# Two standing attention lanes with portioned operand loads in a one-core hybrid decoder layer

## The chip, the core and the metric

One core of one Trainium2 chip runs the whole layer in one launch. The metric is the device time of one execution in microseconds; the time before is the median of three executions. The engines are named as the profile names them: PE (TensorE; PEld its weight loads), DVE (VectorE), ACT (ScalarE), POOL (GpSimd), and SP (SyncE), which here only issues DMAs. Each engine works through its own list of instructions in a fixed order and waits where the next one's inputs are not there yet.

## What is computed

One layer on 256 tokens of width 2048. A norm and one wide projection feed two token mixers, whose outputs are gated, projected, merged and projected once more:

```python
h = rmsnorm(x, pre_norm_g[l]); proj = h @ w_in[l]
(a_q, a_k, a_v, a_g, a_lr, b_q, b_k, b_v, b_g, m_a, m_b) = jnp.split(proj, offsets, axis=-1)
o_a = gla_chunked(a_q, a_k, a_v, gk)                 # gated linear attention, 4 heads
y_a = (rmsnorm(o_a) * silu(a_g)) @ w_branch_a[l]
# differential attention, 16 heads, each with two maps of head size 64:
s = einsum('bqhmd,bkhmd->bhmqk', q / 8, k)            # m = 0, 1
p = softmax(where(mask, s, -inf)); w = p[m=0] - lam * p[m=1]; o_b = w @ v
y_b = (rmsnorm(o_b) * (1 - lam_init) * silu(b_g)) @ w_branch_b[l]
merged = sigmoid(m_a) * y_a + sigmoid(m_b) * y_b
x = x + rmsnorm(merged @ w_out[l], post_norm_g[l])
```

## The kernel before

**The stream of weights.** All weights come from DRAM in tiles of 1 MB, called raw, in one written order, `seq`. Each half of a raw tile is split into a rounded part hi (ACT, line 263) and a remainder lo (DVE, line 264), and the products hi*hi, hi*lo and lo*hi are summed on PE (line 451). raw, hi and lo have three buffers each, so a half can be split only when PE has done with the half three places ahead. Before the attention the projections of the first head groups are computed in a long pinned phase, and their queries and keys (heads groups 0 and 1) and the values and gates of all four groups (`gspill`) are spilled to DRAM. After it the order is: the linear mixer's gates, merge gate m01, queries and keys of group 2, m02, group 3, m03, then the branch matrices `y0` and `y1` and the output matrix `o`.

**The attention beside it.** Small work runs as generators in a list `tasks`; `pump(2)`, called after every second half (every tile) of the stream, lets the first two generators take one step each. The last steps of the linear mixer (`gla_scores`, `gla_out`) come first in that list; then come eight `diff_pair` generators, two heads each, group by group. A pair waits until both pairs of the group ahead are done (or until the linear mixer's two outputs are), then loads its operands in one step, waits two steps, and takes five more:

- `scores`: for each of two maps a PSUM bank `bg`; 8 matmuls per head (lines 991, 992) with q2 against kh and kl; DVE adds the causal mask and takes the row maximum (line 996, `prob<-bg`), which empties the bank; ACT takes the exponentials (line 1002);
- `combine` (line 1007 on): DVE forms p0 - lam*p1;
- `turned`: three transposes and a copy; `weighted`: the product with the values, the per-head norm and the gate (lines 1026 to 1039).

Of the two heads of a pair the second is one step behind the first, and the two pairs of a group are one step apart. At the end four transposes (line 1049) turn the result, and `split_out` writes `obh`, `obl` for the matrix `y1`.

**Operands.** q2 holds for map m the rounded queries in one half of the 128 partitions and their remainders in the other half (four DMAs of 64 partitions by `place`); kh and kl hold rounded keys and remainders in both halves (two DMAs each by `twice`). So one matmul of q2 with kh gives two of the four partial products, and one with kl the other two. All of these DMAs, the values (dv) and gates (ub) and the raw tiles go through SP's one queue.

**Buffers.** q2, kh, kl, dv and ub come from a pool of 18 tiles, in which the input x keeps 8 until m03 is done. The tag `bg` has four PSUM banks. A scheduler fixes each engine's order when the program is built.

Of the kernel before, what the change touches and what calls it, by code (L numbers as in the profile page):

```python
# [7 lines left out]
F32R = mybir.dt.float32r  # L8
BF16 = mybir.dt.bfloat16
U8 = mybir.dt.uint8  # L10
AF = mybir.ActivationFunctionType
# [3 lines left out]
P = 128  # L15
# [22 lines left out]
def chunk_plan():  # L38

    plan = [("v0", "two", "w_in", [(6144, RANK), (2048, 2 * VG[0] - RANK)])]  # L40
    at = 2 * VG[0] - RANK
    for g, n in enumerate(VG[2:]):
        plan.append((f"v{g + 2}", "tok", "w_in", [(2048 + at, n)]))
        at += n
    for hf in range(2):
        for name, base in (("k", 1024), ("q", 0)):
            for c in range(4):
                plan.append((f"{name}{hf}{c}", "chan", "w_in", [(base + 512 * hf + P * c, P)]))
    o = 6144 + RANK
    for s in range(2):  # L50
        plan.append((f"set{s}", "set", "w_in", [(o + 10240 + 1024 * s, 1024)]))
    for s in range(2, SETS):
        plan.append((f"set{s}", "set", "w_in", [(o + base + 512 * (s - 2), 512) for base in (4096, 6144)]))
    for g in range(4):
        plan.append((f"ag{g}", "tok", "w_in", [(4096 + 512 * g, 512)]))
        if g + 2 >= SETS:
            plan.append((f"dv{g}", "tok", "w_in", [(o + 4096 + 512 * g, 512)]))
            plan.append((f"bg{g}", "tok", "w_in", [(o + 6144 + 512 * g, 512)]))
# [36 lines left out]
def hybrid_kernel(ctx: ExitStack, tc, xt, xn, preg, postg, w, w2, gkb, glag, lamv, diffg, ident_d, causal_d, lmask_d, out):  # L95
# [36 lines left out]
    def fetch(d, name, make, queue=pool):  # L132
        t = make(list(d.shape), name, d.dtype)
        queue.dma_start(t, d)
        return t
# [5 lines left out]
    def f32(ap):  # L141
        return ap.bitcast(F32)
# [10 lines left out]
    def halves_of(*keys):  # L153
        return [(key, r, h) for key in keys for r in range(len(at[key])) for h in range(2)]

    def heads_order(g):
        values = (f"dv{g}", f"bg{g}") if g + 2 >= SETS else ()
        chans = [] if g in EARLY else [f"{name}{g}{c}" for pair in range(2) for name in ("dq", "dk") for c in (2 * pair, 2 * pair + 1)]
        return halves_of(*values, *chans)

    seq = halves_of("v0", "v2", "v3") + phase_steps()
    seq += halves_of(*(f"ag{g}" for g in range(4)), "m01") + heads_order(0) + heads_order(1) + heads_order(2)
# [493 lines left out]
    gspill = [None] * (2 * SETS)  # L656

    def merge_gate(banks):
        t = u([P, 2, 512], "mgate")
        for b in range(2):  # L660
            act.activation(t[:, b, :], banks[b], AF.Tanh, scale=half_rstd[:, b : b + 1])
        m0.append(spill(t, "mgate"))
# [284 lines left out]
            tasks.append(gla_out(g // 2, gates[g - 1 :]))  # L947


    obh, obl = [], []  # L950

    def place(t, d, m, h):
        sp.dma_start(f32(t[64 * h : 64 * h + 64, m]), d[64 * m : 64 * m + 64])

    def twice(t, d):

        for h in range(2):
            rows = slice(64 * h, 64 * h + 64)
            sp.dma_start(f32(t[rows]), d.rearrange("(m p) i t -> p m i t", m=2))

    def diff_pair(g, pair, values):
        oh, ol = obh[g], obl[g]
        cm = causal.rearrange("p a t -> p (a t)")
        cuts = ((0, P), (P, 3 * P))
        while not {f"pair{g - 1}{p}" if g else f"out{p}" for p in range(2)} <= done:
            yield
        if not values:
            values.extend(fetch(gspill[2 * g + 4 + i], name, u, sp) for i, name in enumerate(("dv", "ub")))
        q2, kh, kl = (u([P, 2, 2, S], name, F32R) for name in ("q2", "kh", "kl"))
        for m in range(2):  # L970
            for h in range(2):
# [5 lines left out]
        vv, uu = values  # L977
        heads_of = [dict(h=2 * pair + i) for i in range(2)]
        og = []

        def scores(w):
            i2 = w["h"] % 2
# [36 lines left out]

        def weighted(w):  # L1020
            h, z, wt = w["h"], w["z"], w["wt"]
            if not og:
                og.append(t2([P, 2, 2, P], "ogb"))
# [17 lines left out]
        one, two = heads_of  # L1041
        for work in (((scores, one),), ((combine, one), (scores, two)), ((turned, one), (combine, two)), ((weighted, one), (turned, two)), ((weighted, two),)):
            for part, w in work:
                part(w)
            yield
        bank = ps("bg")
        for i in range(2):
            for b in range(2):
                pe.transpose(bank[:, P * (2 * i + b) : P * (2 * i + b) + P], og[0][:, i, b, :], ident)
        hi = oh[:, 2 * pair : 2 * pair + 2, :].rearrange("p h t -> p (h t)")  # L1050
        lo = ol[:, 2 * pair : 2 * pair + 2, :].rearrange("p h t -> p (h t)")
        split_out(bank, hi, lo, diffg_s)
        done.add(f"pair{g}{pair}")

    def diff_heads(g):
        values = []
        if g + 2 >= SETS:
            banks = token_major(f"dv{g}", 512, x_ops, 2)
            late_u = u2 if g > 1 else u
            vv = late_u([P, 2, 512], "dv")  # L1060
            for b in range(2):
                act.activation(vv[:, b, :], banks[b], AF.Copy, scale=rstd[:, b : b + 1])
            banks = token_major(f"bg{g}", 512, x_ops, 2)
            uu = late_u([P, 2, 512], "ub")
            for b in range(2):
                gate(banks[b], b, uu[:, b, :])
            values += vv, uu
        make = u2 if g < 2 else u
        obh.append(make([P, 4, S], "obh", F32R))
        obl.append(make([P, 4, S], "obl", F32R))  # L1070
        for pair in range(2):
            for name in () if g in EARLY else ("dq", "dk"):
# [5 lines left out]
            tasks.append(diff_pair(g, pair, values))  # L1078


    def a_ops(kt):
# [8 lines left out]
    for g in range(3):  # L1090
        diff_heads(g)
    merge_gate(token_major("m02", 512, x_ops, 2))
    diff_heads(3)
    merge_gate(token_major("m03", 512, x_ops, 2))
# [180 lines left out]
```

## Time and profile before

| what | value |
|---|---|
| median of three executions | 1111.01 us (1110.8 to 1115.99) |
| the profiled execution itself | 1114.24 us |
| its span, first to last instruction | 1112.5 us |
| mean granted PE clock in it | 0.995 |
| PE busy / DVE / ACT / POOL, share of the span | 99% / 75% / 60% / 11% |
| HBM read / written | 248.40 MB / 25.17 MB |

The profiled execution is one of its own and not one of the three; what lies around its span is 1114.24 - 1112.5 = 1.74 us. A row of a timeline gives start, duration, engine, line, the tile written and read, the count, and in brackets how long the engine had waited and for what. "Busy" counts the time in which an instruction was on the engine; matmuls overlap, so the pace of PE is read from the starts of successive rows.

### The profile page before, as it was taken

Reading aid. Unit: us, or ns where it says so; the run is one execution under the profiler, and the core shown is the slowest. Engines: PE = TensorE matmul, PEld = TensorE weight load, DVE = VectorE, ACT = ScalarE, POOL = GpSimd, SP = SyncE. Lnnn points to the kernel's source line nnn. Section 1 sums busy time; section 2 is a strip of 40 time slices with the busy share of each in tenths; the row PEclk is TensorE's granted clock in tenths of the full one; section 3 lists DMA queues with packets and bytes.
Section 4 is the critical chain, followed back from the end, with each engine's and each line's share of the span. In section 5 each row is a group of like instructions: output and inputs, shape, how many; then the busy total and the mean of one; then the engine's idle time right before and its main releaser. Section 6 shows DMA issues by size and latency. Waiting matters only on the chain.

```text
span 1112.5 us, 15209 instructions
## 1 busy us (share of the span) xinstructions
PE 1098.4 (99%) x5546; PEld 943.9 (85%) x5546; DVE 839.3 (75%) x1176; ACT 666.9 (60%) x975; POOL 120.7 (11%) x185
## 2 busy tenths in 40 slices
PE   9999999999999999999999999999999899999997
PEld 8999888888888888888888888889888788888886
DVE  7797977979979889799898757758675655656463
ACT  7885766666666766667555455747574643444460
POOL 0201111121121210220100001011100010000000
PEclk9999999999999999999999999999999899999999
DMA  9869879699797897984845679869949575556752
GB/s 346 291 227 327 279 267 306 163 302 295 276 304 205 318 252 256 317 243 157 331 158 184 222 244 288 260 214 304 297 171 263 200 282 189 189 189 212 272 196 77
DMA packets 57884, 274.56 MB, mean 247 GB/s; under 512 B 7440, under 2 KB 8976, under 8 KB 38352
## 3 DMA queue, kind: packets, MB, share of 16 engines
q1 hardware_dynamic: 37536, 192.57, 49.7%
q0 software_dynamic: 19264, 79.70, 25.2%
q10 hardware_dynamic: 1008, 1.32, 0.4%
q8 instruction: 43, 0.70, 0.2%
q14 instruction: 33, 0.27, 0.1%
HBM read 248.40 MB, written 25.17 MB: 246 GB/s over the span
## 4 chain that ended last, share of the span: by engine, by line
PE 97%; ACT 1%; DVE 1%; issue 1%; DMA 0%; DVEq 0%; SPq 0%; POOLq 0%; POOL 0%; ACTq 0%
PE mm L451 66%; PE bg L451 19%; PE bg L439 2%; PE mm L424 2%; PE mm L439 2%; PE bg L870 1%; PE bg L424 1%; PE bg L992 1%; PE bg L991 1%; DMA raw<-in_w_dram 0%; PE bg L1016 0%; PE bg L1027 0%; PE bg L1028 0%; PE bg L1026 0%; PE bg L1124 0%
## 5 line engine op out<-in xcount | busy, mean ns | idle before, releaser
L263 ACT ACTIVATE hi<-raw 128x1024 fp32r<-128x1024 f32 (+3 forms) x291 | 299.6, 1032 | 319.9 <-PE mm L451 216.9
L264 DVE TENSOR_TENSOR lo<-raw,hi 128x1024 fp32r<-128x1024 f32 (+3 forms) x291 | 345.3, 1190 | 179.5 <-ACT hi L263 176.5
L451 PE MATMUL mm<-hi,xs 128*128 128x512 f32 (+1 forms) x864 | 217.3, 387 | 0.3 <-ACT hi L263 0.3
L451 PEld LDWEIGHTS mm<-hi,xs 128*128 128x128 f32 x864 | 159.7, 188 | 27.1 <-ACT hi L263 0.7
L451 PE MATMUL bg<-xs,hi 128*128 128x512 f32 x512 | 131.9, 389 | 0.0
L264 DVE TENSOR_TENSOR lo<-a,hi 128x1024 fp32r<-128x1024 f32 x96 | 115.7, 1220 | 8.1 <-ACT hi L263 7.0
L451 PE MATMUL mm<-lo,xs 128*128 128x512 f32 (+1 forms) x432 | 119.1, 384 | 0.1
L263 ACT ACTIVATE hi<-a 128x1024 fp32r<-128x1024 f32 x96 | 101.7, 1060 | 22.8 <-PE mm L451 20.4
L451 PEld LDWEIGHTS bg<-xs,hi 128*128 128x128 f32 x512 | 96.2, 188 | 18.7
L451 PEld LDWEIGHTS mm<-lo,xs 128*128 128x128 f32 x432 | 80.9, 188 | 15.1 <-DVE lo L264 0.4
L451 PEld LDWEIGHTS bg<-xs,lo 128*128 128x128 f32 x512 | 69.8, 190 | 5.0
L451 PE MATMUL bg<-xs,lo 128*128 128x256 f32 x512 | 71.4, 282 | 0.0
L451 PE MATMUL mm<-xs,hi 128*128 128x512 f32 x256 | 66.9, 394 | 0.0
L264 DVE TENSOR_TENSOR lo<-b,hi 128x1024 fp32r<-128x1024 f32 x48 | 57.8, 1221 | 7.4 <-ACT hi L263 6.6
L263 ACT ACTIVATE hi<-b 128x1024 fp32r<-128x1024 f32 x48 | 50.8, 1060 | 15.6 <-PE mm L451 13.8
L451 PE MATMUL mm<-hi,oah 128*128 128x512 f32 x128 | 52.0, 406 | 3.0 <-ACT hi L263 3.0
L451 PEld LDWEIGHTS mm<-xs,hi 128*128 128x128 f32 x256 | 46.2, 189 | 7.8
L451 PE MATMUL mm<-hi,oal 128*128 128x512 f32 x128 | 51.1, 399 | 0.0
L451 PE MATMUL mm<-hi,obh 128*128 128x512 f32 x128 | 50.4, 394 | 0.0
L451 PE MATMUL mm<-hi,obl 128*128 128x512 f32 x128 | 49.9, 390 | 0.0
L1002 ACT ACTIVATE prob<-prob,mx,score_scale 128x128 f32<-128x128 f32 x64 | 34.1, 534 | 15.9 <-DVE mx L997 15.9
L451 PE MATMUL mm<-hi,mh 128*128 128x512 f32 x96 | 37.5, 390 | 0.0
(286 smaller groups left out, 1866.1 us busy)
## 6 DMA issues: line engine op xcount, KB each, us to landing
raw<-in_w_dram SPq DMA_DIRECT2D x128, 1024.0 KB, 5.3
a<-in_w_dram POOLq DMA_DIRECT2D x24, 512.0 KB, 12.7
c<-in_w_dram SPq DMA_DIRECT2D x24, 512.0 KB, 8.7
b<-in_w_dram POOLq DMA_DIRECT2D x24, 512.0 KB, 9.1
raw<-in_w_dram SPq DMA_DIRECT2D x14, 832.0 KB, 7.1
a<-in_w_dram POOLq DMA_DIRECT2D x10, 1024.0 KB, 5.2
b<-in_w_dram POOLq DMA_DIRECT2D x10, 1024.0 KB, 7.8
dh<-dh POOLq DMA_DIRECT2D x16, 256.0 KB, 4.3
```

The source lines that it names most:

```text
L263: act.activation(hi_t[:, a:b], r[:, a:b], AF.Copy)
L264: dve.tensor_tensor(out=lo_t[:, a:b], in0=r[:, a:b], in1=f32(hi_t[:, a:b]), op=ALU.subtract)
L424: i = pe.matmul(out, lhs, rhs, start=first and n == 0, stop=last and n == len(pairs) - 1)
L439: i = pe.matmul(banks[g][b][:, :n], a[part][:, P * b : P * b + P], w[:, n * g : n * g + n], start=first, stop=last)
L451: i = pe.matmul(*args, **kw)
L870: pe.matmul(o, xk[:, P * c : P * c + P], xq.rearrange("p (b c t) -> p b c t", b=2, c=4)[:, :, c, :], start=i == 0, stop=i == 1)
L991: pe.matmul(banks[m][:, lo:up], q2[:, m, i2, t], kh[:, m, i2, :n], start=True, stop=False)
L992: pe.matmul(banks[m][:, lo:up], q2[:, m, i2, t], kl[:, m, i2, :n], start=False, stop=True)
L1002: act.activation(prob[m][:, lo:up], prob[m][:, lo:up], AF.Exp, scale=score_scale[:, b : b + 1], bias=mx[:, i : i + 1], accum_out=z[:, i : ...
```

## The change

The eight pairs become two generators, `diff_lane(0)` and `diff_lane(1)`, one for each pair of every group, which live through all four groups:

- Each lane has one q2, one kh and one kl for good, and clears one half of kl per map once (POOL memset). Into kl only the half that meets the rounded queries is loaded, so the product of remainder with remainder is left out of the scores. A pair has then 4 + 4 + 2 = 10 DMAs of 64 partitions and 128 KB, 1.25 MB; it had 4 of 128 KB and 4 of 256 KB, 1.5 MB.
- After the second head's scores the lane is given the three portions "q", "kh", "kl" of the next group, and `arrive` loads one of them at each of the next steps.
- A lane does not wait for the other lane or for the group to be done. The transposes of a group's result (`turned_out`) run at the start of the next group's first step; the five-step pairs of a lane follow each other directly.
- dv is fetched in that first step and ub in the second, by lane 0. Merge gates m01 to m03 come from another pool, and `obh`, `obl` are made only when they are needed.
- The branches for groups that are computed late, which never applied with `SETS = 6`, are gone. The matrix products and their order in the stream stay as they were.

```diff
+    def diff_lane(pair):
...
+        while not {"scores1", "out0"} <= done:
+            yield
         q2, kh, kl = (u([P, 2, 2, S], name, F32R) for name in ("q2", "kh", "kl"))
         for m in range(2):
-            for h in range(2):
-                place(q2, heads[g, pair, "dq"][h != m], m, h)
-        for t, d in zip((kh, kl), heads[g, pair, "dk"]):
-            twice(t, d)
-        yield
-        yield
+            pool.memset(f32(kl[64 - 64 * m : P - 64 * m, m]), 0.0)
+        missing = []
+        def arrive(g):
+            if not missing or (g, pair, "dk") not in heads:
+                return
+            part = missing.pop(0)
+            for m in range(2):
+                for h in range(2):
+                    if part == "q":
+                        place(q2, heads[g, pair, "dq"][h != m], m, h)
+                    elif part == "kh":
+                        place(kh, heads[g, pair, "dk"][0], m, h)
+                    elif h == m:
+                        place(kl, heads[g, pair, "dk"][1], m, h)
...
+        for g in range(4):
...
+            one, two = (dict(g=g, h=2 * pair + i) for i in range(2))
+            if pair == 0:
+                values[g] = [fetch(gspill[2 * g + 4], "dv", u, sp)]
+            if g:
+                turned_out(g - 1)
+            scores(one)
+            yield
+            if pair == 0:
+                values[g].append(fetch(gspill[2 * g + 5], "ub", u, sp))
+            combine(one)
+            scores(two)
+            yield
+            missing += ("q", "kh", "kl") if g < 3 else ()
+            for work in (((turned, one), (combine, two)), ((weighted, one), (turned, two)), ((weighted, two),)):
+                arrive(g + 1)
+                for part, w in work:
+                    part(w)
+                yield
+        turned_out(3)
+    tasks.extend(diff_lane(pair) for pair in range(2))
```

What the scheduler makes of it shows at three places. (The changed program's lines are numbered 5 lower in the stream's functions, 3 lower where a tile is fetched, and 7 lower in `scores`; numbers behind a name tell tiles apart.)

**SP, the operands of the last group.** Before, in the middle of `y0`, 18 DMAs stand between the raw tiles 7898 and 7943: one of dv, and the 17 shown here, ub and the two pairs' q, kh and kl:

```order
L134 DMA ub_7879<-gr_4702 128x1024
L953 DMA q_752_7881<-dh_6873 64x512
L953 DMA q_752_7881<-dl_6875 64x512 x2
L953 DMA q_752_7881<-dh_6873 64x512
L959 DMA kh_7882<-dh_7062 64x2x512 x2
L959 DMA kl_7883<-dl_7064 64x2x512 x2
L953 DMA q_759_7932<-dh_7227 64x512
L953 DMA q_759_7932<-dl_7229 64x512 x2
L953 DMA q_759_7932<-dh_7227 64x512
L959 DMA kh_7933<-dh_7371 64x2x512 x2
L959 DMA kl_7934<-dl_7373 64x2x512 x2
L226 DMA raw_7943<-in_w_dram 128x2048
```

Now the same group's operands (dv, and the lanes' q, kh and kl) stand around the last tiles of m03 and the first one of `y0`, 7653, a portion of each lane at a time:

```order
L131 DMA dv_7687<-gl_4789 128x1024
L221 DMA raw_7504<-in_w_dram 128x2048
L948 DMA q_488_6140<-dh_6924 64x512
L948 DMA q_488_6140<-dl_6926 64x512 x2
L948 DMA q_488_6140<-dh_6924 64x512
L948 DMA kh_6141<-dh_7105 64x512 x4
L221 DMA raw_7577<-in_w_dram 128x2048
L948 DMA q_497_6206<-dh_7296 64x512
L948 DMA q_497_6206<-dl_7298 64x512 x2
L948 DMA q_497_6206<-dh_7296 64x512
L948 DMA kl_6142<-dl_7107 64x512 x2
L221 DMA raw_7653<-in_w_dram 128x2048
```

The last two portions follow behind 7653. The largest number of operand DMAs between two raw tiles is now 14, at group 2. The last group is through 14 halves (7 tiles) of the stream earlier than before.

**ACT, the last group's exponentials.** Before, in the middle of `y0`, the splits of tile 7943 stood behind seven exponentials of two heads (763 and 764 are the two maps of the one, 771 and 772 of the other):

```order
L1002 ACTIVATE prob_763_7977,z_7980<-prob_763_7977,mx_7979,score_scale 128x128
L1002 ACTIVATE prob_763_7977,z_7980<-prob_763_7977,mx_7979,score_scale 128x256
L1002 ACTIVATE prob_764_7978,z_7980<-prob_764_7978,mx_7979,score_scale 128x128
L1002 ACTIVATE prob_764_7978,z_7980<-prob_764_7978,mx_7979,score_scale 128x256
L1002 ACTIVATE prob_771_8039,z_8042<-prob_771_8039,mx_8041,score_scale 128x128
L1002 ACTIVATE prob_771_8039,z_8042<-prob_771_8039,mx_8041,score_scale 128x256
L1002 ACTIVATE prob_772_8040,z_8042<-prob_772_8040,mx_8041,score_scale 128x128
L263 ACTIVATE hi_7961<-raw_7943 128x1024
L263 ACTIVATE hi_8002<-raw_7943 128x1024
```

Now this group meets the end of m03 and the first tiles of `y0` (7653, 7738). Their splits 7740 and 7756 stand behind the first head's four exponentials, of which two rows are shown, and ahead of the second head's (735):

```order
L995 ACTIVATE prob_723_7699,z_7701<-prob_723_7699,mx_7700,score_scale 128x128
L995 ACTIVATE prob_723_7699,z_7701<-prob_723_7699,mx_7700,score_scale 128x256
L258 ACTIVATE hi_7740<-raw_7653 128x1024
L258 ACTIVATE hi_7756<-raw_7738 128x1024
L656 ACTIVATE mgate_7832<-mm_7502,half_rstd 128x512
L656 ACTIVATE mgate_7832<-mm_7503,half_rstd 128x512
L498 ACTIVATE obh_7694<-bg_7802,diffg_s 128x512
L995 ACTIVATE prob_735_7779,z_7782<-prob_735_7779,mx_7781,score_scale 128x128
```

Between the two heads' exponentials stand two splits, the merge gate and a result's hi part, where before nothing stood.

**PE and DVE, two heads' scores in one step.** Before, at group 2, the scores of two heads followed each other on PE in four banks, 7522, 7523, 7545 and 7546:

```order
L992 MATMUL bg_7522<-kl_7359,q_674_7357 128x256
L991 MATMUL bg_7523<-kh_7358,q_674_7357 128x256
L992 MATMUL bg_7523<-kl_7359,q_674_7357 128x256
L991 MATMUL bg_7545<-kh_7412,q_683_7411 128x128
L992 MATMUL bg_7545<-kl_7413,q_683_7411 128x128
L991 MATMUL bg_7546<-kh_7412,q_683_7411 128x128
L992 MATMUL bg_7546<-kl_7413,q_683_7411 128x128
```

Now, at group 3, a bank of transposes (7802) stands between them, so the step uses five; with four banks the fifth, 7814, is one that 7783 or 7784 has left:

```order
L985 MATMUL bg_7783<-kl_6142,q_488_6140 128x256
L984 MATMUL bg_7784<-kh_6141,q_488_6140 128x256
L985 MATMUL bg_7784<-kl_6142,q_488_6140 128x256
L1039 MATMUL bg_7802<-ident,ogb_7632 128x128 x4
L984 MATMUL bg_7813<-kh_6207,q_497_6206 128x128
L985 MATMUL bg_7813<-kl_6208,q_497_6206 128x128
L984 MATMUL bg_7814<-kh_6207,q_497_6206 128x128
```

At group 1 the order is the same, but the fifth bank (6903) comes behind all four matmuls of the fourth (6902) and four of the stream; at group 2 likewise, with six of the stream:

```order
L1039 MATMUL bg_6891<-ident,ogb_6693 128x128 x4
L984 MATMUL bg_6902<-kh_6207,q_497_6206 128x128
L985 MATMUL bg_6902<-kl_6208,q_497_6206 128x128
L984 MATMUL bg_6902<-kh_6207,q_497_6206 128x256
L985 MATMUL bg_6902<-kl_6208,q_497_6206 128x256
L446 MATMUL mm_6929<-xs_75,hi_6743 128x512 x2
L446 MATMUL mm_6929<-xs_76,hi_6743 128x512 x2
L984 MATMUL bg_6903<-kh_6207,q_497_6206 128x128
```

On DVE at group 3 the reductions that empty banks 7783 and 7784 stand behind two splits of weights:

```order
L259 TENSOR_TENSOR lo_7741<-raw_7653,hi_7740 128x1024
L259 TENSOR_TENSOR lo_7757<-raw_7738,hi_7756 128x1024
L989 ISA prob_735_7779,mx_7781<-bg_7783,causal 128x128
L989 ISA mx_7781 128x1
L989 ISA prob_735_7779,mx_7781<-bg_7783,causal 128x256
```

At groups 1 and 2 one split and one small operation on queries or keys stand there. PE has 3784 rows in both programs, with the same matmuls.

More of the change, by code (lines that the diff above doesn't have):

```diff
@@ L1021, in weighted @@
             h, z, wt = w["h"], w["z"], w["wt"]
-            if not og:
-                og.append(t2([P, 2, 2, P], "ogb"))
+            if h % 2 == 0:
+                og[:] = [t2([P, 2, 2, P], "ogb")]
+            vv, uu = values[w["g"]]
             bank = ps("bg")
@@ L1039, in weighted @@
                 dve.scalar_tensor_tensor(out=og[0][:, h % 2, b, :], in0=bank[:, P * b : P * b + P], scalar=e[:, b : b + 1], in1=uu[:, b, hv], op0=ALU.mult, op1=ALU.mult)
[L1041 to L1044, printed above, removed]
-            yield
[L1046 to L1053, printed above, removed]
-    def diff_heads(g):
[L1056 to L1070, printed above, removed]
+        def turned_out(g):
+            bank = ps("bg")
+            for i in range(2):
+                for b in range(2):
+                    pe.transpose(bank[:, P * (2 * i + b) : P * (2 * i + b) + P], og[0][:, i, b, :], ident)
+            if len(obh) == g:
+                make = u2 if g < 2 else u
+                obh.append(make([P, 4, S], "obh", F32R))
+                obl.append(make([P, 4, S], "obl", F32R))
+            hi = obh[g][:, 2 * pair : 2 * pair + 2, :].rearrange("p h t -> p (h t)")
+            lo = obl[g][:, 2 * pair : 2 * pair + 2, :].rearrange("p h t -> p (h t)")
+            split_out(bank, hi, lo, diffg_s)
@@ new lines, in diff_lane @@
+        for g in range(4):
+            if g == 0:
+                missing += "q", "kh", "kl"
+            late = len(missing)
+            while missing:
+                arrive(g)
+                yield
+            if late:
+                yield
+            while "out1" not in done:
+                yield
[5 more added lines that the diff above has]
+            scores(one)
+            yield
+            if pair == 0:
[8 more added lines that the diff above has]
+                    part(w)
+                yield
@@ L1089, in hybrid_kernel @@
     merge_gate(token_major("m01", 512, x_ops, 2))
-    for g in range(3):
-        diff_heads(g)
+    diff_heads(2)
     merge_gate(token_major("m02", 512, x_ops, 2))
```

27 lines of the change are left out of this document (5 added, 22 removed).

## Prediction, made before the changed kernel ran

> **What bounds the kernel now.** I read the page first: the busy shares, the slices, the chain that ended last.
>
> ```profile
> span 1112.5 us, 15209 instructions
> PE 1098.4 (99%) x5546; PEld 943.9 (85%) x5546; DVE 839.3 (75%) x1176; ACT 666.9 (60%) x975; POOL 120.7 (11%) x185
> PE   9999999999999999999999999999999899999997
> PEclk9999999999999999999999999999999899999999
> PE 97%; ACT 1%; DVE 1%; issue 1%; DMA 0%; DVEq 0%; SPq 0%; POOLq 0%; POOL 0%; ACTq 0%
> ```
>
> PE is busy for 1098.4 of 1112.5 us and holds 97% of the chain; DMA holds none of it. Only one slice of forty before the last, number 32 (about 862 to 890 us), shows PE below nine tenths, and there its clock is lower too. The change keeps every matmul, so whatever it gains must come out of PE's idle time and of that clock. Next come the waits of PE alone (waiting line, releaser: us in total, times, longest), and the stretches around slice 32 (length, then busy time of PE, PEld, DVE, ACT and POOL with counts, PE clock, DMA share, GB/s):
>
> ```profile
> PE mm L451 <- ACT hi L263: 3.4, 2, 3.0
> PE bg L345 <- DVE ones_b L342: 1.6, 1, 1.6
> PE bg L439 <- ACT hi L263: 0.7, 1, 0.7
> ```
>
> ```profile
> 840.00:860.00 20.00, 20.00 (x96) 16.71 (x95) 10.73 (x23) 7.89 (x15) 1.79 (x3) 1.00 1.06 293
> 860.00:880.00 20.00, 16.95 (x76) 14.03 (x75) 14.25 (x47) 11.12 (x25) 0.00 (x0) 0.83 0.69 261
> 880.00:900.00 20.00, 20.00 (x109) 17.15 (x108) 12.20 (x28) 12.54 (x35) 3.53 (x6) 1.00 0.52 182
> ```
>
> Of the long stream one wait is left: 3.05 us for a rounded half, hi. Its neighbours have none. The timeline shows who was late, and the chain what PE lost behind it:
>
> ```profile
> 864.13 0.28 PE L992 MATMUL bg<-kl,q 128*128 128x256 f32 x1
> 864.81 0.49 ACT L1002 ACTIVATE prob<-prob,mx,score_scale 128x128 f32<-128x128 f32 x1 [4.24 <-DVE mx L997]
> 866.37 1.99 ACT L263 ACTIVATE hi<-raw 128x1024 fp32r<-128x1024 f32 x2
> 867.46 0.79 PE L451 MATMUL mm<-hi,oah 128*128 128x512 f32 x1 [3.05 <-ACT hi L263]
> ```
>
> ```profile
> 857.11 5.47 PE mm L451 x24
> 867.46 8.59 PE mm L451 x24
> ```
>
> ACT was idle for 4.24 us, but its next instruction was an exponential that waited for the row maxima of the last group's scores; the split that PE wanted stood behind three of them (front: ACT's rows). Afterwards 24 matmuls of one kind took 8.59 us, where the same 24 took 5.47 us before: 3.12 us more, with a granted clock of 0.83 in that stretch. So this place costs 3.05 + 3.12 = 6.17 us in the profiled execution.
>
> The Trainium skill, "TensorE: Matmul & The Clock Gate", section "Part 1: The HAM clock gate", says that the array falls to half rate after an idle window of about 3.4 us, that the windows run freely, and that the cost differs from run to run. The trace agrees with a slow stretch behind an idle of 3.05 us, and no idle here is long enough to test the figure. By that rule some executions pay the 3.12 and others do not.
>
> The raw tile was late as well. SP's queue (start, us in all, count) and the landing of the three raw tiles that SP issued from 855.75 on (us from issue):
>
> ```profile
> 837.69 0.42 SPq L134 DMA_DIRECT2D dv<-gl  x1
> ...
> 855.75 1.49 SPq L226 DMA_DIRECT2D raw<-in_w_dram  x3
> ```
>
> ```profile
> DMA to landing us min/median/max: 9.2/11.0/13.0
> ```
>
> The 18 operand DMAs of the group (4 MB) hold the queue from 837.69 to 855.75, 18.06 us; the raw tile behind them lands at 855.75 + 9.2 = 864.95 at the earliest. One split takes 1.99/2 = 1.0 us, so without the exponentials PE could have gone on at about 866.0, still 1.6 us late.
>
> **The change, part by part.** *The stall.* Both of its causes go. On SP the longest run of operand DMAs between two raw tiles falls from 18 to 14, and none of the 14 is larger than 128 KB except dv. At the pace of this block, 18.06/18 = 1.0 us, 14 take 14 us; at the duration of one issue less:
>
> ```profile
> 838.68 0.64 SPq L953 DMA_DIRECT2D q<-dh  x1
> ```
>
> At 0.64 they take 9 us. So the raw tile comes 4 to 9 us earlier than in the old block, and 1.6 us were missing. On ACT the last group's splits 7740 and 7756 now stand ahead of the second head's exponentials. The group also ends seven tiles earlier, so nothing is packed into the middle of y0. I take the whole 3.05 away and with it the 3.12. Bounds: 3.05 (+3.12) if both causes go, 3.05 - 1.6 = 1.45 if raw is as late as before.
>
> *Ten DMAs a pair in place of eight.* 16 more in all, 2 MB less.
>
> ```profile
> raw<-in_w_dram SPq DMA_DIRECT2D x128, 1024.0 KB, 5.3
> ...
> kh<-dh SPq DMA_DIRECT2D x16, 256.0 KB, 7.0
> ...
> q<-dh SPq DMA_DIRECT2D x16, 128.0 KB, 6.7
> ```
>
> 16 x 0.64 = 10 us more of SP's issuing, spread over the length of four groups, behind it only the raw tiles. A portion of four lands some 4 x 0.64 + 6.7 = 9 us after it is begun; a step is one raw tile's work on PE, 2 x (5.47 us and a little) = 11 us or more, and the first portion has three steps, the last one or two. PE pays 0 for it while a raw tile lands ahead of its split; its cover is the three raw buffers. If that cover were gone, the 10 us would be the price in the worst case, and I give that little weight, since DMA holds 0% of the chain.
>
> The Trainium skill, "SBUF — State Buffer", section "The DMA setup-cost knee", speaks against more and smaller transfers: every DMA pays a fixed 2 us or so whatever its size. The rows agree that size hardly matters, 6.7 us for 128 KB and 7.0 us for 256 KB. By an estimate from that page 16 transfers would cost 32 us one after another; several are under way at once here, so the sum would not change while the queue has time.
>
> *Clearing of kl.* Four memsets on POOL, which is 11% busy, once and before the first portion. 0. The product of kl keeps its shape, so PE gains nothing from the zeros.
>
> *Merge gates and obh/obl in other pools, dead branches.* No instruction more or less on PE, DVE or ACT. 0; the cover is that the pools have room when they are asked.
>
> *Two lanes that run on: five banks in one step.* This is the new wait. At groups 1 to 3 lane 0's scores (2 banks), lane 1's transposes (1) and lane 1's scores (2) fall into one step, and `bg` has four. PE must wait with the fifth bank until DVE has read the first. Before, that never happened, so I bound it by the old step at group 2, where two heads' scores follow each other and DVE works on two splits meanwhile:
>
> ```profile
> 810.06 2.35 DVE L264 TENSOR_TENSOR lo<-raw,hi 128x1024 fp32r<-128x1024 f32 x2
> 810.10 0.22 PE L991 MATMUL bg<-kh,q 128*128 128x128 f32 x1
> ...
> 810.27 0.27 PE L991 MATMUL bg<-kh,q 128*128 128x128 f32 x1
> ...
> 811.02 0.22 PE L991 MATMUL bg<-kh,q 128*128 128x128 f32 x1
> ...
> 812.89 0.08 DVE L996 DVE_READ_ACCUMULATOR2_ANT mx<- 128x1 f32 x1
> ```
>
> ```profile
> 844.68 0.60 PE L1049 MATMUL bg<-ident,ogb 128*128 128x128 f32 x4
> 845.03 0.47 PE L451 MATMUL mm<-hi,oah 128*128 128x512 f32 x1
> ```
>
> The first head's scores take 811.02 - 810.10 = 0.92 us on PE, its first bank is read out at 812.89 + 0.08 = 812.97, that is 2.87 us after they began. Four transposes move PE on by 845.03 - 844.68 = 0.35. At group 3 two small matmuls of the fourth bank come next (810.27 - 810.10 = 0.17), and PE is at the fifth bank after 0.92 + 0.35 + 0.17 = 1.44 us: it waits 2.87 - 1.44 = **1.4**. At group 1 the whole fourth bank (half of the 0.92) and four stream matmuls (24 take 5.47, so 0.23 each) come in between: 0.92 + 0.35 + 0.46 + 0.92 = 2.65, a wait of **0.2**. At group 2 six of them: 3.11, **0**. Sum 1.6 us. It is 0 where DVE has got its splits behind it when the scores come. If DVE's split begins one operation later than in this row (2.35/2 = 1.18 us) at all three places, it is 2.6 + 1.4 + 0.9 = 4.9. I take 1.6, since the front's rows of DVE at group 3 are those of the step that I read. Behind the waiting matmul stands the whole stream on PE; ACT and DVE run on, so nothing is late next to it.
>
> *The sum.* Against the profiled execution: 1114.24 - 3.05 - 3.12 + 1.6 = 1109.7. The median, 1111.01, lies 3.23 below the profiled time, which is about the 3.12 of the slow clock: I read the median as an execution with the wait and without the slow matmuls. From it: 1111.01 - 3.05 + 1.6 = **1109.6 us**. I forecast that, 0.1% below before.
>
> **The rivals.** A change counts from 0.5% on, about what a measurement of this kernel can tell from none: 1105.5 and 1116.6.
>
> *The bank waits are covered.* 1111.01 - 3.05 = 1108.0. For it: at groups 1 and 2 only one split stands ahead of the reductions. Against: two stand there at group 3. Either way it is no change by the bound.
>
> *The stall stays, or a like one comes elsewhere*, so that the change does not do what it says. Portions still share SP's queue with raw, now 14 in a row at group 2; with raw 1.6 us late as before, 1111.01 - 3.05 + 1.6 + 1.6 = 1111.2, and with one slow stretch 1114.3. Against it: 4 to 9 us earlier, and ACT waited for a raw tile only five times:
>
> ```profile
> ACT hi L263 <- DMA raw<-in_w_dram: 5.2, 5, 1.7
> ```
>
> *Slower: short waits for a bank take the clock down.* Each of the three five-bank steps would be followed by a slow stretch like the one at 867.46: 3 x 3.12 = 9.4, so 1109.6 + 9.4 = 1119.0. One or two of them, 1112.7 and 1115.8, would stay below 1116.6; it decides from three. For it: the one wait of the trace that lies in the stream was followed by such a stretch. Against: it was 3.05 us long, and mine are 1.4 and less; the wait of 0.7 us in the list left no slice of the clock below nine tenths. The Trainium skill, same page, section "A second HAM failure mode: psum-queue depth-cycling", tells of such a case, where short idles between groups of matmuls on cycled banks throttle the array. Whether one short idle does so, no run here shows.
>
> *Faster by 0.5%.* It would take 5.6 us, and the median holds only 3.05 us of stall. It needs a gain in matmul pace that the profile does not show.
>
> **How the numbers follow.** Forecast 0.60, banks covered 0.13, stall in another place 0.14, slow clock by bank waits 0.08, faster 0.05. The range begins at 1107.3, the covered case less three times the 0.21 us by which the lowest of the three runs (1110.8) lies under their median, and ends at 1114.3, the case with raw late and one slow stretch; that takes in the upper bound of the bank waits (1111.01 - 3.05 + 4.9 = 1112.9) and leaves out the case of three slow stretches and the gain. Chances: faster 0.05, same 0.87, slower 0.08.
>
> **What would show it.** Right: no wait for hi of 3 us in PE's list, slice 32 at nine tenths in both rows, and in PE's waits a line of `bg` (its L984) released by DVE, 0.5 to 2 us in all, most of it in m03's last steps. The raw tiles behind portions land without ACT waiting for them longer than 1.7 us. Wrong: a wait of PE for hi or lo behind portions; bank waits of over 3 us; a clock below nine tenths behind a wait of 1.4 us or less; or a PE busy time that differs from 1098.4 by more than the lost slow stretch.

## The result and the profile after

The changed kernel takes **1110.28 us** (median of 20 executions, 1109.67 to 1112.08). Over 20 executions of its own the kernel before has a median of 1114.05 us (1110.8 to 1116.86); the 1111.01 of the three runs that stood ahead of the prediction, which are among the 20, lies at the fast end of that. The ratio is 0.9967, with a 95% interval of 0.996 to 0.9975: 0.33% faster, inside the 0.5% that the prediction counted as no change. The profiled execution of the changed kernel is 1110.26 us, 3.98 below the profiled one of before.

The page of the changed kernel; in the slices, the dip of slice 32 in PE and in PEclk is gone:

```profile
span 1108.5 us, 15246 instructions
PE 1095.9 (99%) x5546; PEld 941.8 (85%) x5546; DVE 837.2 (76%) x1176; ACT 666.8 (60%) x975; POOL 123.5 (11%) x189
PE   9999999999999999999999999999999999999997
PEclk9999999999999999999999999999999999999998
PE 96%; DVE 1%; ACT 1%; issue 1%; DMA 0%; POOL 0%; DVEq 0%; SPq 0%; POOLq 0%; ACTq 0%
```

PE has the same 5546 matmuls and is busy 2.5 us less; the slow stretch that is missing was 3.12. Its list of waits (waiting line, releaser: us in total, times, longest) shows the exchange that was forecast: the 3.05 us for hi are out, three waits for a bank are in.

```profile
PE bg L984 <- DVE mx L989: 1.7, 3, 0.8
PE bg L340 <- DVE ones_b L337: 1.6, 1, 1.6
PE bg L434 <- ACT hi L258: 0.8, 1, 0.8
PE mm L446 <- ACT hi L258: 0.3, 1, 0.3
```

The three in the timeline, at groups 1 and 2 with the first score and what DVE does ahead of the bank, at group 3 with what stands around it (start, us, engine, line, tiles, and the wait ahead in brackets):

```profile
751.27 0.22 PE L984 MATMUL bg<-kh,q 128*128 128x128 f32 x1
...
752.57 1.23 DVE L259 TENSOR_TENSOR lo<-raw,hi 128x1024 fp32r<-128x1024 f32 x1 [0.30 <-ACT hi L258]
...
754.60 0.09 DVE L989 DVE_READ_ACCUMULATOR2_ANT mx<- 128x1 f32 x1
...
754.74 0.33 PE L984 MATMUL bg<-kh,q 128*128 128x128 f32 x1 [0.55 <-DVE mx L989]
```

```profile
788.61 0.22 PE L984 MATMUL bg<-kh,q 128*128 128x128 f32 x1
...
789.90 1.22 DVE L259 TENSOR_TENSOR lo<-raw,hi 128x1024 fp32r<-128x1024 f32 x1
...
792.26 0.08 DVE L989 DVE_READ_ACCUMULATOR2_ANT mx<- 128x1 f32 x1
...
792.40 0.33 PE L984 MATMUL bg<-kh,q 128*128 128x128 f32 x1 [0.43 <-DVE mx L989]
```

```profile
824.84 2.35 DVE L259 TENSOR_TENSOR lo<-raw,hi 128x1024 fp32r<-128x1024 f32 x2
...
825.35 0.22 PE L984 MATMUL bg<-kh,q 128*128 128x128 f32 x1
825.41 0.28 PE L985 MATMUL bg<-kl,q 128*128 128x128 f32 x1
...
826.27 0.60 PE L1039 MATMUL bg<-ident,ogb 128*128 128x128 f32 x4
826.62 0.31 PE L984 MATMUL bg<-kh,q 128*128 128x128 f32 x1
...
827.66 0.09 DVE L989 DVE_READ_ACCUMULATOR2_ANT mx<- 128x1 f32 x1
...
827.80 0.33 PE L984 MATMUL bg<-kh,q 128*128 128x128 f32 x1 [0.76 <-DVE mx L989]
827.87 0.09 DVE L989 DVE_READ_ACCUMULATOR2_ANT mx<- 128x1 f32 x1
...
827.97 0.27 PE L985 MATMUL bg<-kl,q 128*128 128x128 f32 x1
```

At group 3 DVE goes through two splits (2.35 us) before it reads the first bank; PE does scores, transposes and two small matmuls meanwhile, and stands for 0.76 us until 827.80. At groups 1 and 2 only one split stands there, but it begins 1.3 us behind the first score. The windows of the same stretches as before (length, busy time of PE, PEld, DVE, ACT, POOL, PE clock, DMA share, GB/s) have no gap and no slow clock:

```profile
840.00:860.00 20.00, 20.00 (x109) 17.15 (x108) 13.74 (x31) 11.52 (x29) 5.15 (x9) 1.00 0.57 189
860.00:880.00 20.00, 20.00 (x92) 16.57 (x91) 10.15 (x11) 8.12 (x8) 1.43 (x3) 1.00 0.89 340
```

### The profile page after: what moved, and what is told of

It reads as the page before. It is cut to its first block, busy times and chain, and to the rows that moved or that the text cites. A ratio compares the mean times of both kernels' runs of the same rounds, so it can differ in the third digit from the quotient of the medians.

```text
span 1108.5 us, 15246 instructions
## 1 busy us (share of the span) xinstructions
PE 1095.9 (99%) x5546; PEld 941.8 (85%) x5546; DVE 837.2 (76%) x1176; ACT 666.8 (60%) x975; POOL 123.5 (11%) x189
## 4 chain that ended last, share of the span: by engine, by line
PE 96%; DVE 1%; ACT 1%; issue 1%; DMA 0%; POOL 0%; DVEq 0%; SPq 0%; POOLq 0%; ACTq 0%
PE mm L446 66%; PE bg L446 20%; PE bg L434 2%; PE mm L419 2%; PE mm L434 2%; PE bg L865 1%; PE bg L419 1%; PE bg L984 1%; PE bg L985 0%; DMA raw<-in_w_dram 0%; PE bg L1009 0%; DVE lo L259 0%; PE bg L1133 0%; PE bg L925 0%; PE bg L1021 0%
```

## Experiments

The theory: a split of a raw tile that stands behind exponentials on ACT, or a raw tile that is late, makes PE wait; an idle of some us brings slow matmuls; the change removes this one place and pays with three bank waits. The rivals: fewer bytes, the place of the last group, the lanes as such. Ratios are against the kernel before on the same chip, with 95% intervals; "PE waits" are those in the stream behind the first 100 us.

| kernel | median us (range, executions) | ratio | PE waits in its profile, us |
|---|---|---|---|
| changed kernel | 1110.28 (1109.67 to 1112.08, 20) | 0.9967 [0.996, 0.9975] | bank 1.7 in 3 |
| turned_later | 1107.66 (1107.51 to 1109.63, 5) | 0.9946 [0.9933, 0.9958] | none |
| kl_both | 1110.2 (1109.52 to 1111.79, 8) | 0.9977 [0.9968, 0.9987] | bank 1.7 in 3 |
| groups_wait | 1108.57 (1108.39 to 1111.8, 6) | 0.9965 [0.9953, 0.9977] | bank 0.4 |
| all_at_once | 1114.26 (1111.46 to 1117.14, 12) | 1.0011 [0.9999, 1.0022] | bank 1.5 in 2, kl 1.1 |
| before_values_early | 1113.93 (1111.28 to 1115.82, 12) | 0.9998 [0.9987, 1.0009] | hi 3.0 |
| before_half_kl | 1108.2 (1107.22 to 1109.5, 6) | 0.9947 [0.9934, 0.996] | hi 0.2 |
| before_two_portions | 1107.73 (1107.38 to 1110.1, 5) | 0.9956 [0.9944, 0.9968] | none |
| before_split_first | 1111.9 (1109.85 to 1113.84, 12) | 0.9983 [0.9972, 0.9994] | hi 2.2 |
| portions_split_behind | 1114.4 (1112.37 to 1116.16, 12) | 1.0005 [0.9995, 1.0015] | hi 3.1, kl 0.3 |

**before_again: the kernel before once more.** No edit.

> The kernel before, unchanged, for a second profile. If the 3.05 us wait of PE for hi is built into the order of the instructions, it is there again at the same place (2.9 to 3.2 us), and what differs between executions is only the slow stretch behind it: its 24 matmuls take anything from 5.5 to 11 us, and the time lies between 1110.8 and 1116.9. If instead the wait comes and goes with how DMA happens to run, its length differs by over 0.5 us between the two profiles.

1112.61 us. Again PE waits 3.0 us for hi. Its chain, at the place of the 8.59 us:

```profile
856.76 5.47 PE mm L451 x24
...
867.11 7.34 PE mm L451 x24
...
875.69 5.45 PE mm L451 x24
```

The same 24 matmuls took 7.34 us behind an equally long wait, 1.25 less than the 8.59 of the first profile, and the execution was 1.63 shorter. So the wait was the same in both, and most of the difference between these two executions lies in the slow stretch behind it. The mean granted clock on record says the same of 59 further executions of this kernel: all below 1112 us have 0.998, all above 1113.5 us 0.995 or 0.994. From 1111.15 us at 0.998 to 1116.01 at 0.994 the lost clock is, by an estimate from these rounded figures, 0.004 x 1112 = 4.4 of the 4.9 us.

**turned_later: the changed kernel without five banks in a step.**

```diff
             if pair == 0:
                 values[g] = [fetch(gspill[2 * g + 4], "dv", u, sp)]
-            if g:
-                turned_out(g - 1)
             scores(one)
...
             missing += ("q", "kh", "kl") if g < 3 else ()
+            if g:
+                turned_out(g - 1)
```

> The changed kernel, with the transposes of a group's result moved from a lane's first step to its third, so that no step needs more than four banks. Theory bank waits: the three waits of PE for a bank (1.7 us in the profile, 2.5 us with the matmuls that run slower around them) go, nothing takes their place, 1107.8 to 1108.6 us. Rival: the wait moves to the transposes or to another bank of the third step, or hides something else; 1110 as the changed kernel.

1107.66 us, and its list of PE's waits has nothing behind the first 100 us:

```profile
PE bg L340 <- DVE ones_b L337: 1.6, 1, 1.6
PE bg L434 <- ACT hi L258: 0.7, 1, 0.7
PE mm L446 <- ACT hi L258: 0.3, 1, 0.3
PE mm L434 <- ACT hi L258: 0.2, 1, 0.2
```

So the five-bank step costs 1110.28 - 1107.66 = 2.6 us, for 1.7 us of waits (2.4 if each is first compared with the kernel before on its own chip). It is the one loss that the change itself brought, and this version is faster than both kernels.

**kl_both: the changed kernel with both halves of kl.**

```diff
-                    elif h == m:
+                    else:
                         place(kl, heads[g, pair, "dk"][1], m, h)
...
-        for m in range(2):
-            pool.memset(f32(kl[64 - 64 * m : P - 64 * m, m]), 0.0)
```

> The changed kernel, with kl loaded into both halves again (12 DMAs a pair, nothing cleared; the product of remainder with remainder is back in the scores). Rival fewer bytes (the gain is what is not loaded): a good part of the 3.8 us is lost, 1112 to 1114. Theory ACT order and bank waits: nothing changes, 1110 to 1111 us, no wait for hi over 0.5 us, three waits for a bank of 1.5 to 2 us in all.

1110.2 us, the same three waits for a bank, 1.7 us in all; the profiled executions are 1110.33 us here and 1110.26 there. These runs show no gain from the bytes that the half kl leaves out in the lanes: the two intervals of the ratio overlap.

**all_at_once: the changed kernel with the three portions in one step**, three profiles of it.

```diff
-            part = missing.pop(0)
-            for m in range(2):
+            while missing:
+                part = missing.pop(0)
+                for m in range(2):
```

(The body is one step further in.)

> The changed kernel, with the three portions of a lane loaded in one step; up to 20 operand DMAs then stand between two raw tiles on SP. Rival raw late: such a block holds back raw as the 18 did before, a wait for hi or lo of 1 to 3 us behind at least one block, 1111.5 to 1116. Theory ACT order: the splits that PE wants next stand ahead of the exponentials at these places, so no such wait; only bank waits of 1.5 to 2.5 us, 1110 to 1111 us.

1114.26 us, as slow as the kernel before, with a spread of 5.7 us. My theory's 1110 to 1111 failed. The rival had the time, but not the mechanism: PE waited for no split behind a block, but for kl itself.

> The kernel of all_at_once, unchanged, for a second profile: its first one was its fastest execution (1111.46 us of 1111.46 to 1117.14). Theory late operands: in an execution of 1113 us and more the wait of PE for kl (1.1 us in the first profile) is longer by what the time is longer, or a second such wait stands beside it, and the clock stays at 1.00. Rival slow stretch: the waits are as long as in the first profile, within 0.5 us, and the granted clock falls below 0.95 in a stretch behind one of them.

> The same kernel for a third profile, with the same question: longer waits for operands at a clock of 1.00, or the same waits and a slow stretch behind one of them.

1113.69 and 1113.1 us. Waits and windows of the second profile:

```profile
PE bg L986 <- DMA kl<-dl: 2.2, 1, 2.2
PE bg L340 <- DVE ones_b L337: 1.6, 1, 1.6
PE bg L985 <- DVE mx L990: 1.5, 2, 0.8
```

```profile
800.00:820.00 20.00, 17.77 (x103) 15.61 (x102) 15.21 (x48) 13.36 (x35) 3.93 (x6) 0.96 0.79 253
820.00:840.00 20.00, 20.00 (x98) 16.89 (x98) 13.02 (x41) 13.77 (x35) 1.29 (x2) 0.95 0.44 158
```

and the chain ahead of that wait:

```profile
808.03 5.43 DMA dl<-dk
...
813.48 5.20 DMA kl<-dl
...
818.72 0.47 PE bg L986
```

kl is read back from dl, the copy of the keys' remainders in DRAM, and dl itself landed only at 808.03 + 5.43 = 813.46 us. SP issued kl right behind it, and PE stood for 2.2 us until kl was there. The step with both lanes' scores of group 3 begins here at 814.90 us, in the changed kernel at 825.35: a lane takes one step for each portion that is missing (`while missing: arrive(g); yield`), so with all three in one step it comes to its scores earlier, before its keys are back. So the portions do more than keep blocks in SP's queue short: they give the keys time. That this distance alone makes the loss is a reading of the chain; no run loaded all at once and kept the scores where they were.

Each theory of the expectation held by half: from the first to the second profile the wait for kl grew from 1.1 to 2.2 us (to 1.8 in the third), half or less of what the time grew, and the clock fell from 1.00 to 0.95 behind it, in both.

**groups_wait: the lanes with the old order of groups.**

```diff
-            if g:
-                turned_out(g - 1)
...
+            turned_out(g)
+            done.add(f"pair{g}{pair}")
+            while not {f"pair{g}{p}" for p in range(2)} <= done:
+                yield
-        turned_out(3)
```

> The changed kernel, but a lane waits after each group until the other lane is done too, and writes its result out at the end of its own group, as before; the portions stay. The last group is back in the middle of y0, and a block of 16 operand DMAs stands on SP. Rival place (the gain came from ending the attention earlier): the 3 us wait and its slow stretch are back, 1112 to 1115. Theory ACT order and bank waits: no split that PE wants at once stands behind waiting exponentials, and at most one or two steps need five banks, so 1108 to 1109 us, below the changed kernel.

1108.57 us, with one wait of 0.4 us for a bank. The 16 operand DMAs in a row are there (from 801.88 to 812.77 us) and cost nothing. But the last group is not where the expectation put it: its scores run from 829 to 844 us, at the start of y0, where the kernel before has them at 856 to 877 and the changed kernel at 818 to 835. So this run does not rule out the place; before_two_portions, further down, does.

**before_values_early: the kernel before with dv and ub asked for earlier** (groups 1 to 3).

```diff
+        if g:
+            if not values:
+                values.extend(fetch(gspill[2 * g + 4 + i], name, u, sp) for i, name in enumerate(("dv", "ub")))
         while not {f"pair{g - 1}{p}" if g else f"out{p}" for p in range(2)} <= done:
             yield
```

> The kernel before, with values and gates of a group (dv, ub, 1 MB) asked for before the pair waits for the group ahead; nothing else. In the last group 16 operand DMAs in place of 18 stand between the two raw tiles, so raw lands some 1 to 3 us earlier; ACT's order of the split and the second head's exponentials is as before. Theory ACT order (the split stands behind exponentials that wait for the row maxima): the wait stays at 3.0 us and the time at 1114 (1111 to 1117). Rival raw late (the block in SP's queue holds back the tile): the wait falls below 1.5 us and the time to about 1109 to 1111.

1113.93 us, the wait of 3.0 us. But the trace shows the same 18 DMAs in one block (dv at 839.30, the raw tile at 857.04 us), so the edit did not bring raw forward and tells nothing of it.

**before_half_kl: the kernel before with one half of kl.**

```diff
-        for t, d in zip((kh, kl), heads[g, pair, "dk"]):
-            twice(t, d)
+        twice(kh, heads[g, pair, "dk"][0])
+        for m in range(2):
+            pool.memset(f32(kl[64 - 64 * m : P - 64 * m, m]), 0.0)
+            place(kl, heads[g, pair, "dk"][1], m, m)
```

> The kernel before, with kl loaded into one half only (other half cleared per pair); pairs, waits and loads in one step stay. SP's block in the last group is still 18 DMAs, 3.5 in place of 4 MB; by the order of instructions both splits of the raw tile behind the block now stand ahead of the second head's exponentials on ACT. Theory ACT order: the 3.05 us wait goes or falls to the 1.6 us and less by which raw is late, 1108 to 1110 us, without the five-bank waits. Rival raw late: a wait of 1.5 to 3 us stays and with it the slow stretch, 1112 to 1115. Rival fewer bytes: as ACT order in time, but then the loading of both halves in the lanes must cost the same 4 us.

1108.2 us. The block has still 18 DMAs, yet the wait is down to 0.22 us. SP and ACT at that place:

```profile
854.94 12.45 SPq L226 DMA_DIRECT2D raw<-in_w_dram  x4
...
863.59 2.01 ACT L263 ACTIVATE hi<-raw 128x1024 fp32r<-128x1024 f32 x2 [2.95 <-PE bg L994]
...
864.70 0.50 PE L451 MATMUL mm<-hi,oah 128*128 128x512 f32 x1 [0.22 <-ACT hi L263]
```

Two things changed at once. The raw tile landed 8.5 us after 854.94, at 863.44, 1.5 us earlier than in the kernel before; and ACT took the split at 863.59, ahead of the second head's exponentials (the bracket names a matmul of the scores that ended at the same time). With kl_both it follows that the gain here is not one of bytes as such. Which of the two it was, the next three runs tell.

**before_two_portions: the kernel before with the keys one step later.**

```diff
                 place(q2, heads[g, pair, "dq"][h != m], m, h)
+        yield
         for t, d in zip((kh, kl), heads[g, pair, "dk"]):
             twice(t, d)
         yield
-        yield
```

> The kernel before, with q2 (and values, gates) loaded in the pair's first step and kh, kl one step later; else unchanged: full kl, eight pairs, last group in the middle of y0. The longest block on SP is 14, and by the order of instructions both splits of the tile behind it stand ahead of the second head's exponentials on ACT. Theory ACT order: the wait is gone, 1107.5 to 1109 us. Rival lanes (only the standing tiles and early loads help): 1112 to 1115 as before.

1107.73 us, and no wait in the stream. The last group's scores run from 856 to 870 us, where the kernel before begins them too. So no lane, no earlier end of the attention and no half kl is needed for the gain; one `yield` gives all of it and spares the bank waits. Here too raw comes earlier and the split stands ahead, on SP and ACT:

```profile
851.49 0.33 SPq L226 DMA_DIRECT2D raw<-in_w_dram  x1
...
860.08 1.99 ACT L263 ACTIVATE hi<-raw 128x1024 fp32r<-128x1024 f32 x2
865.02 0.49 ACT L1002 ACTIVATE prob<-prob,mx,score_scale 128x128 f32<-128x128 f32 x1 [2.95 <-DVE mx L997]
```

**before_split_first and portions_split_behind: order and raw apart.** The first is the kernel before, with only this:

```diff
+                    with tc.issue_after(held[0] if held and (g, w["h"]) == (3, 1) else latest[0]):
-                    act.activation(prob[m][:, lo:up], prob[m][:, lo:up], AF.Exp, ...)
+                        act.activation(prob[m][:, lo:up], prob[m][:, lo:up], AF.Exp, ...)
```

(`held` is the split of y0's tile, `("y01", 3, 0)`.) The second is before_two_portions with the reverse; `held` is there the third exponential, and the split is written behind it:

```diff
+            with (tc.issue_after(held[0]) if held and e == ("y01", 3, 0) else contextlib.nullcontext()):
-            act.activation(hi_t[:, a:b], r[:, a:b], AF.Copy)
+                act.activation(hi_t[:, a:b], r[:, a:b], AF.Copy)
...
         while emitted[0] < min(j + 1 + AHEAD, len(seq)):
+            if seq[emitted[0]] == ("y01", 3, 0) and emitted[0] > j:
...
+                break
             emit_half()
```

> The kernel before, with only ACT's order changed at one place: the exponentials of the last group's second head must come behind the split of the raw tile that PE wants next (hi_7961). The block of 18 operand DMAs on SP is as before, so raw is as late as before. If order and late raw each carry a part, as the prediction said (1.45 and 1.6 of the 3.05 us), the wait of PE falls to 1.6 us (1.2 to 2), or to 0.5 if raw lands 1 us earlier in this execution; time 1108.5 to 1112, a slow stretch possible. Theory order alone: the wait falls below 0.4 us, 1107.5 to 1108.5. Rival raw alone: 3.05 us stay, 1111 to 1117.

> The kernel of before_two_portions (raw in time, no wait, 1107.7 us), with only ACT's order changed at the same place: the split of that raw tile must come behind the third exponential of the last group's second head (all four come ahead of it in the order). If the order alone is enough for the wait, PE waits 3 to 3.6 us for hi with raw in time, and the time is 1111 to 1117 with a slow stretch of 0 to 6 us as in the kernel before. Rival raw: no wait, 1107.5 to 1108.5.

1111.9 and 1114.4 us. The split in the first kernel, and the exponentials and the split in the second:

```profile
865.88 2.00 ACT L264 ACTIVATE hi<-raw 128x1024 fp32r<-128x1024 f32 x2 [4.93 <-DMA raw<-in_w_dram]
866.99 0.80 PE L454 MATMUL mm<-hi,oah 128*128 128x512 f32 x1 [2.20 <-ACT hi L264]
```

```profile
866.30 0.59 ACT L1011 ACTIVATE prob<-prob,mx,score_scale 128x256 f32<-128x256 f32 x1
...
866.89 2.94 ACT L266 ACTIVATE hi<-raw 128x1024 fp32r<-128x1024 f32 x3
867.98 0.80 PE L460 MATMUL mm<-hi,oah 128*128 128x512 f32 x1 [3.06 <-ACT hi L266]
```

In the first, ACT waits for the raw DMA itself, and PE for 2.20 us. In the second the raw tile was asked for at 851.34 us, 4.4 earlier than the 855.75 of before, and landed 8.0 us later, 7.5 us ahead of its split; PE waits 3.06 us all the same, because the split stands behind exponentials. So **each of the two causes is enough alone**: late raw for about 2.2 us, the order for 3.06; and where both are mended (before_two_portions) there is none. The part of raw was above the forecast 1.6, since the tile landed at 856.23 + 9.5 = 865.7 us, 0.9 us after PE had run out of work (866.99 - 2.20 = 864.8), where it was 0.5 in the first profile. In before_again it was 1.5 (855.69 + 9.9 = 865.6 against 864.1), so there late raw alone would have made 2.8 of the 3.0 us, by an estimate with the 1.3 us that lie between landing and PE's start in before_split_first. Together they cost 1113.11 - 1107.73 = 5.4 us, the wait and its slow stretch, by the medians of before_two_portions and the kernel before on its chip.

## Why the prediction was right

The time, 1110.28, lies in the range of 1107.3 to 1114.3, 0.7 above the forecast of 1109.6, and the change is within 0.5%. By its steps:

- **The stall: right, and for the reason given.** The 3.05 us and the slow matmuls are gone, and the crossed runs confirm both causes. The split into 1.6 for raw and the rest for the order was a reading of one execution; the parts do not add up, since the later of the two sets the end, and raw's own part was 2.2 us where it was measured alone.
- **The slow stretch: right in size, wrong in the median.** I took the median of three, 1111.01, for an execution without the slow matmuls. Twenty executions gave 1114.05: by the clocks of the further executions the slow stretch is in most of them, with a length that varies. So the change is worth 3.8 us by the medians, and I expected 1.4. The time is met all the same, since 1111.01 and the changed kernel's 1110.28 are both times without the stretch; the size of the change is not. The sum against the profiled execution, which held the stretch, came to 1109.7 and met 1110.26.
- **The five-bank waits: the mechanism right, the sizes not.** Forecast 0.2, 0 and 1.4 at groups 1, 2, 3, in all 1.6; measured 0.55, 0.43 and 0.76, in all 1.7. That the sums agree is luck. I took one old step for all three places, with two splits that begin with the scores and a bank that is read out 2.87 us after they began. At group 3 DVE began its splits 0.5 us ahead of the scores (824.84 against 825.35), and the bank was read out after 2.4 us. At groups 1 and 2 the one split began 1.3 us behind the first score (752.57 against 751.27, 789.90 against 788.61), small operations on queries and keys came between it and the bank, and the bank was read out after 3.4 and 3.7 us. And a wait costs more than its idle time: turned_later puts the three at 2.6 us. The idle time is counted from the end of the matmul ahead, while PE would have started the next one before that end. By the starts of the matmuls, which stand 0.11 to 0.23 us apart without a wait, the three places lose some 2.2 us, an estimate; and behind the wait at group 3 the second matmul starts 827.97 - 827.80 = 0.17 us after the first and not 825.41 - 825.35 = 0.06. This term, sized 1.6 for 2.6, is the one that was off in the sum against the profiled execution; with 2.6 that sum is 1110.7, and the 0.4 by which it lies above 1110.26 stays open.
- **More and smaller DMAs, clearing of kl, pools: 0, right.** kl_both is within 0.1 us of the changed kernel, and no wait of PE names an operand. The cover was thinner than I thought, though: with the portions in one step (all_at_once) it is gone, by 4 us. I had priced it as raw that comes late; it was kl, which had to wait until its own keys had landed in DRAM.
- **The rivals.** Banks covered (1108.0) is what turned_later shows, 1107.66, and not what happened. The stall in another place did not come. Slow clock by bank waits did not come at 0.8 us; but the clock fell behind a wait of 1.8 us in all_at_once, well below the 3.05 us that I had seen.

Open: some executions of kernels without a long wait lie 1.5 to 3 us above the rest (1110.1 in before_two_portions, 1111.8 in groups_wait, 1111.65 to 1112.08 in three of the changed kernel's 20). No profile caught one. The first two have a mean granted clock of 0.998, within 0.001 of their faster fellows, so a slow stretch does not explain them; the changed kernel's three have 0.997, where the others have 0.997 to 0.999.

## What to carry to other kernels

Where one engine is busy for 99%, look for the one place where it stands, and ask which instruction is ahead of the late one on its own engine: here it was a split behind exponentials on ACT and a weight tile behind 18 small loads on SP, and mending one of the two alone leaves a wait of 2.2 or 3.1 us. A block of small loads in the queue of the weights can do harm twice, by the late weight and by the order that a scheduler makes of it, and spreading it over one more step (one `yield`) was worth more than the whole rewrite. When loads are moved together, ask whether their data are back in DRAM by then. When generators are merged, count the PSUM banks that one step asks for: the fifth of four cost 2.6 us.

## What the runs showed of the hardware

Matmuls slowed down behind idle times of PE below 3 us too. Behind 2.2 us (before_split_first) the 24 matmuls took 8.59 us, as behind 3.05; behind 2.2 and 1.8 us in all_at_once the granted clock was 0.95 to 0.96 in the two windows of 20 us at that place, and behind 1.1 us, in its first profile, 1.00. It was 1.00 behind 1.45 us too, 8 us after the start of groups_wait and of before_half_kl; between 1.45 and 1.8 us no profile has an idle time between two matmuls. In the slow stretch of the kernel before, matmuls of 128x512 started 0.43 us apart, where 0.23 is usual. The stretch need not begin with the end of the wait: in before_again the third and the fourth matmul still started 0.23 us after the ones ahead. Behind the same wait of 3.0 us the cost differs from execution to execution, 8.59, 7.34 and 8.30 us for the 24 matmuls (the first profile, before_again, before_values_early). By the clocks given with before_again this makes most of the spread of the kernel before, 6 us; the kernels without a wait of over 1 us have a spread of 2 to 3.5.
